# A planner's durations and yields rewritten for a streaming encoder layer: VectorE work issued in pieces

## The chip, the cores and the metric

The kernel runs on one core of a Trainium2 chip. A core has TensorE (PE; its weight loads are listed as PEld), VectorE (DVE), ScalarE (ACT), GpSimd (POOL) and SyncE (SP), which here only issues DMAs. Each engine works through its own instructions in order; semaphores make it wait for others. The metric is device time in microseconds (us), lower is better.

## What is computed

One layer on 1024 prompt rows and 64 sample rows of width 1024. A normalised input goes through one projection; its columns feed a differential attention (group A, 8 heads) and an RWKV-7 recurrence (group B, 16 heads of 64). Both are gated and go through one output projection. Cut to what matters:

```python
h = _rms_norm(x, norm_pre, NORM_EPS)
proj = h @ w_in
q = _partial_rope(proj[..., A_Q:A_K]...); k = _partial_rope(proj[..., A_K:A_V]...); v = proj[..., A_V:A_G]
s = jnp.einsum('bqhcd,bkhcd->bchqk', q, k) * (A_QK_DIM ** -0.5)      # two maps per head
p = jax.nn.softmax(where(visible, s, -inf), axis=-1)
o = (p[:, 0] - lam * p[:, 1]) @ v                                    # then rms norm, gate
ps = proj[..., B_R:B_G]
m = ps + (shifted_by_one_row(ps) - ps) * mu_shift                    # r, k, v, w, a of group B
def step(s, inp):                                                    # per head, state 64 x 64
    sa = jnp.einsum('bhij,bhj->bhi', s, a_t)
    s = s * w_t[:, :, None, :] + sa[..., None] * b_t[:, :, None, :] + v_t[..., None] * k_t[:, :, None, :]
    return s, jnp.einsum('bhij,bhj->bhi', s, r_t)
yb = group_norm(ys) * ln_x_w + ln_x_b + bonus                        # then gate
out = jnp.concatenate([y_a, yb], axis=-1) @ w_out
x_new = x + _rms_norm(out, norm_post, NORM_EPS)
```

## The kernel before

**Work.** The input is normalised and transposed first. Then `phase_b` runs the recurrence in 17 units: a pair of heads and one half of the prompt each (8 pairs x 2 halves), and the sample rows as one unit, put in as the last but one. A unit (`unit`, L485) prepares decays and keys (VectorE products on 128 x 512 tiles, the scan at L563), builds products of the chunks (`m_s`, L643 and L644, masked at L649 to L654), inverts a triangular matrix in five rounds (L690 to L715), then walks its 8 chunks in a serial chain (L812 to L865): a matmul g (L814), a VectorE copy (L828), a matmul u (L831), two copies (L837, L838), a matmul s (L842), and the update of the state in two halves (L852), from which the next chunk starts. Group norm, gate and a store of the result end the unit.

**Fillers.** Beside the units runs one stream of projections (`filler`, L996): 64 weight blocks of 128 columns, each 72 matmuls (`pj`, L215 to L217; every product is made of a high and a low part). Half of them (k, r, v, g for a pair of heads) are inputs of the units; after the matmuls of k, r and v, `shifted` (L362) mixes each row with the one before it, on ScalarE and VectorE. The other half (q, k, v, g of attention heads, `fill_job`, L942) goes to DRAM. `RESERVE` = 6 attention blocks are held back until the pairs are done. When the projections are done and phase B is over, the same stream becomes the output projection (`out_projection`, L1062; `po`, 864 matmuls of 512 columns, of which 216 need all heads).

**Attention.** `phase_a` (L1204) loads each head's q and k, splits them, and per query tile makes scores (`s`, L1361 and L1362, two buffers), the maximum (L1371), exponentials (L1378), transposes (`x_wt`, L1408) and sums (`x_o`, L1422).

**The order.** All of it is issued by `Weave` (L59), a planner that runs when the program is built. Each stream is a generator; it yields nanoseconds to wait or a condition, and `run` picks the lowest rank whose time has come: units by number, fillers at rank 100. TensorE time moves the clock by `spend`; `op` keeps for each other engine when it comes free and returns when its result is there. So a stream that waits longer in the model leaves more places for filler matmuls. Constants before: `LAT` = 100 ns after a matmul, a rate per element and a fixed 80 ns for each operation. Operations of fillers are not booked. The planner's order is then the order in which the instructions are scheduled onto each engine's queue.

Of the kernel before, what the change touches and what calls it, by code (L numbers as in the profile page):

```python
# [27 lines left out]
CH = 64  # L28
# [13 lines left out]
LA, LAT, W_LD, W_DMA = 130, 100, 11000, 3122  # L42
# [4 lines left out]
RS = 1.0  # L47
RATE = {DVE: 1 / 0.96, ACT: 1 / 1.2, POOL: 2.4}

# [6 lines left out]
b_done = [False]  # L56


class Weave:  # L59
# [7 lines left out]
    def __init__(self):  # L67
        self.now = 0.0
        self.live = []
        self.free = {}  # L70
        self.count = itertools.count()

    def spend(self, ns):
# [44 lines left out]
def layer(ctx: ExitStack, tc: tile.TileContext, I, O):  # L118
    nc = tc.nc
# [170 lines left out]
def phase_b(tc, I, O, E):  # L290
# [8 lines left out]
    with ExitStack() as bs:  # L299
# [62 lines left out]
        def shifted(w, idx, tag, dest):  # L362
# [5 lines left out]
        def shift(raw, idx, dest):  # L368
# [5 lines left out]
            for t0, n, d in dest:  # L374
                act(d, raw[:, t0 + 1:t0 + 1 + n], AF.Copy, scale=omu[:, idx:idx + 1])
                if t0 == TP:
                    stt(d[:, 0:1], pc(R_SS + idx), mu, d[:, 0:1], op0=MUL, op1=ADD)
                    stt(d[:, 1:], raw[:, t0 + 1:t0 + n], mu, d[:, 1:], op0=MUL, op1=ADD)
                else:
                    stt(d, raw[:, t0:t0 + n], mu, d, op0=MUL, op1=ADD)  # L380

# [22 lines left out]
        def pair_job(nm, p, w):  # L404
# [10 lines left out]
            if nm == "g":  # L415
                h0, h1 = yield from tiles()

                def evac(ps, t0, n):
                    for s0, s1, d in ((0, HALF, h0), (HALF, TP, h1), (TP, T, gs_[:, p, :])):
# [5 lines left out]
                        stt(d_, d_, 1.0, ps[:, a - t0:b - t0], op0=ADD, op1=MUL)  # L425
                yield from proj_cm(w, evac, f"g{p}")
            else:
# [6 lines left out]
                yield from shifted(w, 8 * j + p, f"{nm}{p}", dest)  # L434
            have.add((nm, p))
# [49 lines left out]
        def unit(n, p, hf):  # L485
# [66 lines left out]
            spend(1100)  # L552
# [10 lines left out]
            nc.vector.tensor_tensor_scan(cs, scm, tw, 0.0, op0=MUL, op1=ADD)  # L563
# [30 lines left out]
            done(op_(DVE, 560))  # L594
# [11 lines left out]
            for h in range(2):  # L606
                r = slice(64 * h, 64 * h + 64)
                vtt(pt[r, :, 2 + h, :], c3(rm)[r], dd[r, :, 1:CH + 1], op=MUL)
                vtt(pt[r, :, h, :], c3(kkn)[r], dd[r, :, 0:CH], op=MUL)
            stt(ta, ta, 1.0, kkn, op0=ADD, op1=MUL)  # L610
            stt(bk[:, :, CH:2 * CH], c3(ta), -0.5, c3(dinv), op0=MUL, op1=MUL)
            gtt(bk[0:64, :, 2 * CH:], c3(kb)[0:64], c3(dinv)[0:64], op=MUL)
            vtt(bk[64:128, :, 0:CH], c3(kb)[64:128], c3(dinv)[64:128], op=MUL)

            vtt(kb, kb, rm, op=MUL)
            op_(DVE, 512)
            free.add(("r", p, hf))
            op_(DVE, 4100)
# [18 lines left out]
            for g in range(2):  # L637
# [7 lines left out]
                spend(1800)  # L645
# [3 lines left out]
                vtt(lt[0:64, gs], pe3[0:64, :, 0:CH], bch(strict[0:64], 4), op=MUL)  # L649
                vtt(lt[64:128, gs], po3[64:128, :, 0:CH], bch(strict[64:128], 4), op=MUL)  # L650
                vtt(pt[64:128, gs, 0, :], pe3[64:128, :, 0:CH], bch(strict[64:128], 4), op=MUL)
                vtt(pt[0:64, gs, 1, :], po3[0:64, :, 0:CH], bch(strict[0:64], 4), op=MUL)
                vtt(rbk[:, gs, 0, :], pe3[:, :, CH:], bch(incl, 4), op=MUL)
                vtt(rbk[:, gs, 1, :], po3[:, :, CH:], bch(incl, 4), op=MUL)  # L654
                yield done(op_(DVE, 6 * 256 + 400), 2)
# [22 lines left out]
            for h in range(2):  # L678
                r = slice(64 * h, 64 * h + 64)
                vtt(c3(xt)[r], lt16[r, :, r], bch(mt[:, 0, :])[r], op=MUL)  # L680
            vtt(c3(xt), c3(xt), bch(id16), op=ADD)
            d = op_(DVE, 800)
            yield d
# [6 lines left out]
            for lv in range(1, 6):  # L690
# [4 lines left out]
                spend(300)  # L695
# [9 lines left out]
                spend(500)  # L705
# [15 lines left out]
            spend(500)  # L721
# [12 lines left out]
            spend(600)  # L734
# [7 lines left out]
            for h in range(2):  # L742
# [5 lines left out]
                spend(500)  # L748
# [27 lines left out]
            spend(500)  # L776
# [35 lines left out]
            for c in range(8):  # L812
# [41 lines left out]
                op_(DVE, 110)  # L854
                if c % 4 == 3:
# [7 lines left out]
                    op_(ACT, 400)  # L863
                    op_(ACT, 400)
                yield op_(DVE, 110)  # L865
# [4 lines left out]
            nc.vector.tensor_reduce(mu, y3, axis=AX.X, op=ADD)  # L870
            vts(mu, mu, -1.0 / CH, None, op0=MUL)
            yc = ycp[:, 0:HALF]
            vtt(c3(yc), y3, bcol(mu), op=ADD)
            yield op_(DVE, 1200)
# [9 lines left out]
            yield op_(POOL, 700)  # L884
# [49 lines left out]
            vtt(yo, yo, gate, op=MUL)  # L934
            if smp:
# [6 lines left out]
        def fill_job(kind, h, w):  # L942
# [3 lines left out]
            def evac(ps, t0, n):  # L946
                if kind == "g":
                    act(st_[:, t0:t0 + n], ps, AF.Tanh, scale=0.5)
                    stt(st_[:, t0:t0 + n], st_[:, t0:t0 + n], 1.0, ps, op0=ADD, op1=MUL)  # L949
                else:  # L950

                    act(st_[:, t0:t0 + n], ps, AF.Copy, scale=0.125 if kind == "q" else 1.0)
            yield from proj_cm(w, evac, f"a{kind}{h}")
# [9 lines left out]
        def rope(kd, g):  # L963
# [16 lines left out]
            for j in range(8):  # L980
# [543 lines left out]
```

## Time and profile before

| | us |
|---|---|
| median of 3 runs (1837.16 to 1842.88) | 1838.92 |
| the profiled execution | 1845.82 |
| its span, first to last instruction | 1844.0 |
| TensorE busy in the span | 1697.7 |
| VectorE busy in the span | 1254.7 |

The span is cut below into stretches by what runs: units and projections until 1229 us, the load of the first attention head until 1268, eight heads until 1714.7, the rest of the output projection. A busy TensorE is counted from the start of a matmul to its modelled end; the clock that is granted to it is in the same rows as a share of 2.4 GHz.

### The profile page before, as it was taken

The numbers are of one execution on the slowest core, as the hardware profiler recorded it, in microseconds if no ns is written. First come the engines' busy times: TensorE is split into PE (matmuls) and PEld (weight loads), VectorE is DVE, ScalarE is ACT, GpSimd is POOL, SyncE is SP. The second block draws the span as 40 slices with busy tenths as digits, with TensorE's granted clock in tenths as the row PEclk, the third lists the DMA queues.
The fourth block names the chain that finished last, engine by engine and source line by source line (L and its number), as shares of the span: only waits on it lengthen the run. The fifth ranks groups of instructions, "written<-read, shape, count | busy, mean of one in ns | idle before, by whom it ended". The sixth has DMA issues, their size and how long they took to land. (4 is left out here: it accounts for less than half of the span.)

```text
span 1844.0 us, 34363 instructions
## 1 busy us (share of the span) xinstructions
PE 1697.7 (92%) x12930; PEld 1516.1 (82%) x12930; DVE 1254.7 (68%) x2583; ACT 846.3 (46%) x2026; POOL 720.6 (39%) x905
## 2 busy tenths in 40 slices
PE   6999899899998999999999899997999988999997
PEld 4888898888888888888888789896889876777876
DVE  5677777778778787787776577643676655776336
ACT  5434444444443344344444334333466566676332
POOL 3542323233233233333333322212245466666663
PEclk8999999999999999999999899998999889999999
DMA  4111111320132111111111121346554654554345
GB/s 153 52 46 37 48 51 51 84 69 27 34 92 61 46 53 33 39 45 31 40 42 52 39 60 54 95 116 178 153 161 132 184 135 121 141 162 120 113 130 164
DMA packets 204096, 158.82 MB, mean 86 GB/s; under 512 B 44085, under 2 KB 185050, under 8 KB 203930
## 3 DMA queue, kind: packets, MB, share of 16 engines
q1 hardware_dynamic: 169098, 137.33, 26.0%
q10 hardware_dynamic: 34832, 19.30, 4.2%
q8 instruction: 102, 1.67, 0.4%
q14 instruction: 64, 0.52, 0.1%
HBM read 108.67 MB, written 47.34 MB: 85 GB/s over the span
## 5 line engine op out<-in xcount | busy, mean ns | idle before, releaser
L1183 PE MATMUL po<-woh,mxh 128*128 128x512 f32 x288 | 120.5, 418 | 2.7 <-ACT woh L157 1.9
L1184 PE MATMUL po<-woh,mxl 128*128 128x512 f32 x288 | 116.0, 403 | 4.1 <-POOL mxl L158 4.1
L1185 PE MATMUL po<-wol,mxh 128*128 128x512 f32 x288 | 115.1, 400 | 3.9 <-POOL wol L158 3.9
L1378 ACT ACTIVATE e<-s,nb 128x128 f32<-128x128 f32 (+7 forms) x144 | 101.1, 707 | 36.3 <-DVE nb L1371 20.5
L821 ACT ACTIVATE sd<-suv,dc 64x64 f32<-64x64 f32 x128 | 44.5, 347 | 151.4 <-DVE suv L852 138.1
L158 POOL TENSOR_TENSOR mxl<-mxr,mxh 128x512 fp32r<-128x512 f32 x63 | 84.5, 1344 | 66.1 <-ACT mxh L157 56.5
L1371 DVE TENSOR_REDUCE nb<-s 128x1 f32<-128x640 f32 (+8 forms) x104 | 95.9, 923 | 2.1
L1422 PEld LDWEIGHTS x_o<-vn,wt 128*128 128x128 f32 (+1 forms) x608 | 80.1, 198 | 15.1 <-ACT wt L1412 5.6
L1422 PE MATMUL x_o<-vn,wt 128*128 128x128 f32 (+1 forms) x608 | 86.5, 287 | 5.4 <-ACT wt L1412 4.1
L1361 PE MATMUL s<-k,qs 128*128 128x512 f32 (+4 forms) x208 | 77.9, 383 | 13.5 <-ACT k L1288 7.4
L842 PE MATMUL cbank<-suv,bkt 128*128 128x128 f32 x256 | 57.6, 307 | 32.0 <-DVE suv L838 31.9
L852 DVE SCALAR_TENSOR_TENSOR suv<-cbank,dc,sd 64x64 f32<-64x64 f32 x224 | 63.1, 282 | 32.7 <-PE cbank L842 28.7
L1194 DVE TENSOR_TENSOR part<-po,part 128x512 f32<-128x512 f32 x54 | 37.2, 689 | 67.2 <-PE po L1185 67.1
L842 PEld LDWEIGHTS cbank<-suv,bkt 128*128 128x128 f32 x256 | 41.9, 192 | 46.2 <-DVE suv L838 44.1
L215 PE MATMUL pj_v<-hhi,wh_v 128*128 128x384 f32 (+1 forms) x192 | 70.9, 369 | 6.2 <-DVE mg L425 5.8
L1362 PE MATMUL s<-k,qs 128*128 128x512 f32 (+4 forms) x208 | 72.0, 363 | 3.4 <-POOL k L1291 2.7
L687 POOL TENSOR_TENSOR ltlo<-lt,lt 64x512 f16<-64x512 f32 x32 | 38.0, 1186 | 93.5 <-ACT lt L675 92.3
L215 PE MATMUL pj_k<-hhi,wh_k 128*128 128x384 f32 (+1 forms) x192 | 67.8, 353 | 4.0 <-ACT raw_k L230 4.0
L215 PE MATMUL pj_r<-hhi,wh_r 128*128 128x384 f32 (+1 forms) x192 | 71.0, 370 | 0.0
L215 PE MATMUL pj_aq<-hhi,wh_aq 128*128 128x384 f32 (+1 forms) x192 | 70.3, 366 | 0.5 <-DVE fl_g L949 0.3
L215 PE MATMUL pj_av<-hhi,wh_av 128*128 128x384 f32 (+1 forms) x192 | 70.0, 364 | 0.7 <-DVE fl_g L949 0.7
L215 PE MATMUL pj_ak<-hhi,wh_ak 128*128 128x384 f32 (+1 forms) x192 | 70.2, 366 | 0.0
(532 smaller groups left out, 6079.7 us busy)
## 6 DMA issues: line engine op xcount, KB each, us to landing
mxr<-mixB SPq DMA_DIRECT2D x32, 256.0 KB
wor<-in_w_out SPq DMA_DIRECT2D x64, 128.0 KB
qa<-scr_q SPq DMA_DIRECT2D x32, 204.0 KB
ka<-scr_k SPq DMA_DIRECT2D x32, 204.0 KB
mxr<-mixA SPq DMA_DIRECT2D x24, 256.0 KB
scr_q<-fl_q SPq DMA_DIRECT2D x8, 544.0 KB
scr_k<-fl_k SPq DMA_DIRECT2D x8, 544.0 KB
scr_v<-fl_v SPq DMA_DIRECT2D x8, 544.0 KB
```

The source lines that it names most:

```text
L158: gtt(lo, raw, hi.bitcast(F32), op=SUB)
L215: mm(ps[:, :n], hi[:, k, :], hhi[i][:, k, :], start=(k == 0), stop=False)
L842: mm(s, bkt[:, c], suv[:, c], start=True, stop=True)
L852: stt(suv[r, c + 1, h, :] if c < 7 and not smp else to[r], s[r, h * CH:(h + 1) * CH], dc[r, c:c + 1], sd[r], op0=MUL, op1=ADD)
L1183: mm(ps, hi[:, q, :], wh, start=(q == 0), stop=False)
L1184: mm(ps, lo[:, q, :], wh, start=False, stop=False)
L1185: mm(ps, hi[:, q, :], wl, start=False, stop=(q == len(ks) - 1))
L1361: mm(s2[:, b:b + w], lq, k1[c][:, k0 + o_:k0 + o_ + w], start=True, stop=False)
L1362: mm(s2[:, b:b + w], lq, k2[c][:, k0 + o_:k0 + o_ + w], start=False, stop=True)
L1371: nc.vector.tensor_reduce(nb[:, 0:m], s3[:, :, 0:n], axis=AX.X, op=MAX, negate=True)
L1378: act(e[:, 0:n], s3[:, j, 0:n], AF.Exp, bias=nb[:, j:j + 1], accum_out=st["sm"][:, c:c + 1])
L1422: mm(ops[:, 0:P], wt[0:w, b, :], vn[0:w, vb, :], start=(b == 0), stop=(b == len(kbs) - 1))
```

## The change

It changes the planner's numbers and the places where streams yield; the operations stay, but for the scan, which becomes two halves, and one GpSimd product that is issued three instructions earlier.

- `LAT` becomes 210 ns, also in attention (`LA`, 130 before). `op` books a fixed part for each engine (`FIX`: 150, 190 and 90 ns) and adds `OUT` = 60 ns to its result. `spend` adds 130 or 105 ns when TensorE goes over to half-height matmuls or back. Several `spend` values change (450 to 1800 ns before; for `m_s` 1800 becomes 1400).
- `near` books an operation and lets the stream wait until VectorE is within 400 ns of it. It follows the single products of the preparation, of the masks, of the inversion's start, of the norm and of the rotation, where several were issued in one go.
- The mix with the row before is a stream of its own at rank 60 (`rest`), at most two of them open, and it yields after each operation. The evacuations of projections are booked.

```diff
-LA, LAT, W_LD, W_DMA = 130, 100, 11000, 3122
+LAT, OUT, W_LD, W_DMA = 210, 60, 11000, 3122
+LA = LAT
+T_IN, T_OUT = 130, 105
+FIX = {DVE: 150, ACT: 190, POOL: 90}
...
-    def op(self, eng, n):
-        self.free[eng] = max(self.now, self.free.get(eng, 0.0)) + RS * (RATE[eng] * n + 80)
-        return self.free[eng] - self.now + (LA if b_done[0] else LAT)
+    def op(self, eng, n, k=1, at=0.0):
+        self.free[eng] = max(self.now + at, self.free.get(eng, 0.0)) + RATE[eng] * n + k * FIX[eng]
+        return self.free[eng] - self.now + OUT
...
             nc.scalar.copy(raw[:, 1 + t0:1 + t0 + n], ps)
+            weave.op(ACT, n, at=LAT)
...
+        def shifted(w, idx, tag, dest, then):
+            yield lambda: len(shifting) < 2
+            shifting.append(tag)
             raw, evac = E["raw_rows"](tag)
             yield from proj_cm(w, evac, tag)
-            yield from shift(raw, idx, dest)
+            def rest():
+                yield from shift(raw, idx, dest, True)
+                shifting.remove(tag)
+                then()
+            weave.add(60, rest())
...
+        def near(eng, n):
+            return max(0.0, op_(eng, n) - OUT - 400)
...
-            nc.vector.tensor_tensor_scan(cs, scm, tw, 0.0, op0=MUL, op1=ADD)
+            nc.vector.tensor_tensor_scan(cs[:, 0:256], scm[:, 0:256], tw[:, 0:256], 0.0, op0=MUL, op1=ADD)
+            yield near(DVE, 512)
+            nc.vector.tensor_tensor_scan(cs[:, 256:], scm[:, 256:], tw[:, 256:], 0.0, op0=MUL, op1=ADD)
...
-                vtt(lt[0:64, gs], pe3[0:64, :, 0:CH], bch(strict[0:64], 4), op=MUL)
-                vtt(lt[64:128, gs], po3[64:128, :, 0:CH], bch(strict[64:128], 4), op=MUL)
...
-                yield done(op_(DVE, 6 * 256 + 400), 2)
+                for i, (o_, s_, m_) in enumerate((
...
+                    vtt(o_, s_, bch(m_, 4), op=MUL)
+                    yield near(DVE, 256) if i < 5 else done(op_(DVE, 256), 2)
```

VectorE, at the first chunks of the chain of unit (0, 1), where the masks of the next unit fall in. `gsb` is the copy of g, `suv` with COPY the copies of u, `suv` with SCALAR_TENSOR_TENSOR the update, `lt`, `pt` and `rbk` from `m_s` the six mask products; `mv` and `vs` are mixes of v, `ysq_o` the end of a unit. Before:

```order
L828 COPY gsb_10_2326<-cbank 128x128
L932 TENSOR_TENSOR ysq_o_0_2299<-ysq_o_0_2299,bv_0_1002 128x512
L380 SCALAR_TENSOR_TENSOR mv_1_2334<-raw_v_2027,pv,mv_1_2334 128x512
L377 SCALAR_TENSOR_TENSOR vs__501<-pv,vs__501 128x1
L378 SCALAR_TENSOR_TENSOR vs__501<-raw_v_2027,pv,vs__501 128x63
L934 TENSOR_TENSOR ysq_o_0_2299<-ysq_o_0_2299,mg_0_996 128x512
L649 TENSOR_TENSOR lt_0_2379<-m_s_00_2381,msk 64x256
L650 TENSOR_TENSOR lt_0_2379<-m_s_01_2382,msk 64x256
L651 TENSOR_TENSOR pt_508<-m_s_00_2381,msk 64x4x64
L652 TENSOR_TENSOR pt_508<-m_s_01_2382,msk 64x4x64
L653 TENSOR_TENSOR rbk_0_2380<-m_s_00_2381,msk 128x4x64
L654 TENSOR_TENSOR rbk_0_2380<-m_s_01_2382,msk 128x4x64
```

After (lines 868, 877, 878, 892, 694 and 402 are 828, 837, 838, 852, 649 to 654 and 380 of before):

```order
L868 COPY gsb_10_2462<-cbank 128x128
L877 COPY suv_1_2395<-cbank 64x64
L878 COPY suv_1_2395<-cbank 64x64
L892 SCALAR_TENSOR_TENSOR suv_1_2395<-cbank,dc_1_1233,sd_10_2459 64x64 x2
L402 SCALAR_TENSOR_TENSOR mv_0_2581<-raw_v_2319,pv,mv_0_2581 128x512
L868 COPY gsb_11_2515<-cbank 128x128
L877 COPY suv_1_2395<-cbank 64x64
L878 COPY suv_1_2395<-cbank 64x64
L694 TENSOR_TENSOR lt_0_2542<-m_s_00_2544,msk 64x256
L694 TENSOR_TENSOR lt_0_2542<-m_s_01_2545,msk 64x256
L892 SCALAR_TENSOR_TENSOR suv_1_2395<-cbank,dc_1_1233,sd_11_2512 64x64 x2
L694 TENSOR_TENSOR pt_508<-m_s_00_2544,msk 64x4x64
```

The six mask products stood in one piece between the copy of g and the copies of u; now they stand in pieces, behind the copies of u, and the update of the chunk goes between them.

TensorE, chunks six and seven of the last unit's chain, pair 7. `cbank` is g, u or s by its operands (`pt`, `xtf`, `bkt`), `y` the outputs. Before:

```order
L831 MATMUL cbank<-gsb_16_15098,xtf 128x128
L215 MATMUL pj_ak_1_15104<-hhi_174,wh_ak_14868 128x384
L216 MATMUL pj_ak_1_15104<-hlo_177,wh_ak_14868 128x384
L217 MATMUL pj_ak_1_15104<-hhi_174,wl_ak_14869 128x384
L215 MATMUL pj_ak_1_15104<-hhi_174,wh_ak_14868 128x384
L216 MATMUL pj_ak_1_15104<-hlo_177,wh_ak_14868 128x384
L217 MATMUL pj_ak_1_15104<-hhi_174,wl_ak_14869 128x384
L842 MATMUL cbank<-suv_1_14703,bkt_1_14672 128x128
L843 MATMUL y_14_14996<-suv_1_14703,rbk_1_14045 128x128
```

After (871, 882, 883, 854, 859 are 831, 842, 843, 814, 819 of before):

```order
L871 MATMUL cbank<-gsb_16_16094,xtf 128x128
L882 MATMUL cbank<-suv_1_15892,bkt_1_15861 128x128
L883 MATMUL y_14_16061<-suv_1_15892,rbk_1_15256 128x128
L854 MATMUL cbank<-suv_1_15892,pt_508 128x128
L859 MATMUL y_14_16061<-suv_1_15892,pt_508 128x128
L871 MATMUL cbank<-gsb_17_16108,xtf 128x128
L882 MATMUL cbank<-suv_1_15892,bkt_1_15861 128x128
L883 MATMUL y_14_16061<-suv_1_15892,rbk_1_15256 128x128
L937 MATMUL m_sto_10_16133<-ident,st_1_16115 64x128
L1317 MATMUL x_ck_16342<-ident,ck_455 128x128
```

The projections between the chain's matmuls are gone there; from the second chunk of this chain on none is left.

TensorE in the seventh attention head, from its first transpose. `x_wt` are transposes, `s` scores, `x_o` sums, `po` the output projection. Before:

```order
L1408 MATMUL x_wt_00_19758<-ident,e_000_19696 128x128
L1183 MATMUL po_19947<-woh_19561,mxh_19632 128x512
L1408 MATMUL x_wt_10_19761<-ident,e_100_19707 128x128 x2
L1184 MATMUL po_19947<-woh_19561,mxl_19633 128x512
L1446 MATMUL x_z_7_19789<-ident,on_4_19437 128x128 x3
L1361 MATMUL s_30_19784<-k_19518,qs_19485 128x512
L1362 MATMUL s_30_19784<-k_19548,qs_19485 128x512
L1361 MATMUL s_30_19784<-k_19585,qs_19550 128x512
L1362 MATMUL s_30_19784<-k_19610,qs_19550 128x512
```

After (1454, 1380, 1468, 1407, 1408 are 1408, 1334, 1422, 1361, 1362 of before):

```order
L1454 MATMUL x_wt_00_20714<-ident,e_000_20662 128x128
L1380 MATMUL x_kt_20716<-ident,ka_20139 128x64 x8
L1468 MATMUL x_o_0_20737<-vn_20151,wt_0_20713 128x128
L1407 MATMUL s_30_20744<-k_20579,qs_20575 128x512
L1408 MATMUL s_30_20744<-k_20596,qs_20575 128x512
L1407 MATMUL s_30_20744<-k_20611,qs_20598 128x512
L1408 MATMUL s_30_20744<-k_20624,qs_20598 128x512
L1454 MATMUL x_wt_10_20751<-ident,e_100_20673 128x128 x2
L1454 MATMUL x_wt_80_20800<-ident,e_800_20727 64x128
```

The output projection's matmuls no longer stand between the head's own. By head, from its first `x_vn` to that of the next, the matmuls of projections and of output projection were 231 + 0, 141 + 0, 120 + 0, 12 + 24, 0 + 84, 0 + 105, 0 + 75, 0 + 78 before, with 498 behind the last `x_o`; they are 0 + 192, 0 + 96, 0 + 108, 0 + 81, 0 + 90, 0 + 81, 0 + 0, 0 + 0 after, with 216 behind it.

## Rows read from the trace of the kernel before

**Rows 1.** The page's first part: busy us, share of the span, instructions.

```profile
PE 1697.7 (92%) x12930; PEld 1516.1 (82%) x12930; DVE 1254.7 (68%) x2583; ACT 846.3 (46%) x2026; POOL 720.6 (39%) x905
```

**Rows 2.** Busy time by stretch: length, then PE, PEld, DVE, ACT, POOL busy (instructions), clock, DMA.

```profile
100.00:1190.00 1090.00, 1025.94 (x9118) 932.71 (x9116) 819.63 (x1759) 454.38 (x1035) 342.22 (x408) 0.99 0.18 51
1190.00:1268.00 78.00, 65.54 (x399) 63.47 (x398) 31.09 (x79) 24.47 (x52) 15.70 (x16) 0.91 0.57 144
1268.00:1347.90 79.90, 73.54 (x434) 66.64 (x434) 48.38 (x101) 38.35 (x100) 33.73 (x40) 0.91 0.59 159
1347.90:1401.00 53.10, 52.04 (x351) 47.52 (x350) 34.10 (x68) 33.15 (x88) 26.70 (x38) 1.00 0.53 144
1401.00:1448.10 47.10, 46.99 (x323) 43.22 (x322) 32.91 (x69) 30.69 (x84) 19.97 (x31) 1.00 0.48 127
1448.10:1504.40 56.30, 45.27 (x243) 36.98 (x242) 33.48 (x70) 34.59 (x95) 30.77 (x41) 0.79 0.55 161
1504.40:1560.40 56.00, 48.43 (x289) 39.64 (x288) 34.16 (x68) 37.34 (x103) 34.87 (x47) 0.98 0.60 153
1560.40:1618.70 58.30, 54.32 (x312) 44.92 (x311) 38.76 (x75) 33.08 (x90) 36.26 (x48) 0.96 0.49 131
1618.70:1666.60 47.90, 46.15 (x282) 38.20 (x281) 36.27 (x69) 35.92 (x98) 33.08 (x42) 1.00 0.56 153
1666.60:1714.70 48.10, 44.98 (x273) 37.72 (x272) 32.09 (x65) 32.36 (x94) 31.55 (x47) 0.96 0.41 122
1714.70:1844.00 129.30, 116.27 (x504) 94.42 (x502) 54.54 (x71) 41.36 (x95) 70.11 (x76) 0.96 0.45 139
```

**Rows 3.** Waits of PE among the units, 100 to 1190 us: total, times, longest.

```profile
PE cbank L842 <- DVE suv L838: 31.9, 34, 3.4
PE cbank L831 <- DVE gsb L828: 10.0, 12, 1.8
```

**Rows 4.** Timeline, 205 to 208 us: start, us, engine, line, what [idle before, releaser].

```profile
205.18 0.41 DVE L649 TENSOR_TENSOR lt<-m_s,msk 64x256 f32<-64x256 f32 x1
...
207.38 0.21 DVE L837 COPY suv<-cbank 64x64 f32<-64x64 f32 x1
207.60 0.23 DVE L838 COPY suv<-cbank 64x64 f32<-64x64 f32 x1
207.88 0.49 PE L842 MATMUL cbank<-suv,bkt 128*128 128x128 f32 x2 [2.40 <-DVE suv L838]
```

**Rows 5.** Busy time by stretch, 1100 to 1190 us.

```profile
1100.00:1190.00 90.00, 89.26 (x831) 82.12 (x823) 58.75 (x135) 34.63 (x86) 18.80 (x17) 1.00 0.22 63
```

**Rows 6.** Timeline, end of the last chain to the first score.

```profile
1227.73 0.38 PE L831 MATMUL cbank<-gsb,xtf 128*128 128x128 f32 x2
1228.22 0.22 DVE L837 COPY suv<-cbank 64x64 f32<-64x64 f32 x1 [1.28 <-PE cbank L831]
...
1228.92 0.38 PE L842 MATMUL cbank<-suv,bkt 128*128 128x128 f32 x2
1229.35 0.58 DVE L852 SCALAR_TENSOR_TENSOR st<-cbank,dc,sd 64x64 f32<-64x64 f32 x2 [0.65 <-PE cbank L842]
...
1244.71 0.35 SPq L938 DMA_DIRECT2D mixB<-ysq_o  x1
...
1264.45 0.80 PE L1361 MATMUL s<-k,qs 128*128 128x128 f32 x2 [6.66 <-ACT k L1288]
```

**Rows 7.** Timeline of PE, two projection and two output matmuls that follow each other.

```profile
1179.80 0.34 PE L215 MATMUL pj_ak<-hhi,wh_ak 128*128 128x384 f32 x1
1179.97 0.34 PE L216 MATMUL pj_ak<-hlo,wh_ak 128*128 128x384 f32 x1
...
1715.25 0.39 PE L1183 MATMUL po<-woh,mxh 128*128 128x512 f32 x1
1715.47 0.39 PE L1184 MATMUL po<-woh,mxl 128*128 128x512 f32 x1
```

**Rows 8.** Busy time by stretch, 1452 to 1482 us.

```profile
1452.00:1482.00 30.00, 23.70 (x115) 18.32 (x113) 21.32 (x49) 18.86 (x54) 11.63 (x20) 0.77 0.75 225
```

More of the change, by code (lines that the diff above doesn't have):

```diff
@@ L70, in __init__, with spend @@
         self.free = {}
+        self.part = False
         self.count = itertools.count()
-    def spend(self, ns):
+    def spend(self, ns, part=False):
+        if part != self.part:
+            self.part = part
+            ns += T_IN if part else T_OUT
         self.now += ns
-    def op(self, eng, n):
-        self.free[eng] = max(self.now, self.free.get(eng, 0.0)) + RS * (RATE[eng] * n + 80)
-        return self.free[eng] - self.now + (LA if b_done[0] else LAT)
+    def op(self, eng, n, k=1, at=0.0):
+        self.free[eng] = max(self.now + at, self.free.get(eng, 0.0)) + RATE[eng] * n + k * FIX[eng]
+        return self.free[eng] - self.now + OUT
     def later(self, ns, call):
@@ L425, in evac @@
                         stt(d_, d_, 1.0, ps[:, a - t0:b - t0], op0=ADD, op1=MUL)
+                        op_(DVE, b - a, at=op_(ACT, b - a, at=LAT))
                 yield from proj_cm(w, evac, f"g{p}")
+                have.add((nm, p))
             else:
@@ L433, in dest @@
                     return [(0, HALF, h0[:, o_:o_ + HALF]), (HALF, HALF, h1[:, o_:o_ + HALF]), (TP, TS, samp)]
-                yield from shifted(w, 8 * j + p, f"{nm}{p}", dest)
-            have.add((nm, p))
+                yield from shifted(w, 8 * j + p, f"{nm}{p}", dest, lambda: have.add((nm, p)))
         def t512(tag="t", bufs=5, dt=F32, nm=""):
@@ L586, in unit @@
                 stt(kkn, km, pc(R_KK + p), psb, op0=MUL, op1=MUL)
+            yield near(DVE, 560)
+            done(0)
             kb = t512(nm=f"kb{u}")
@@ L608, in unit @@
                 vtt(pt[r, :, 2 + h, :], c3(rm)[r], dd[r, :, 1:CH + 1], op=MUL)
+                yield near(DVE, 512)
                 vtt(pt[r, :, h, :], c3(kkn)[r], dd[r, :, 0:CH], op=MUL)
+                yield near(DVE, 512)
+            gtt(bk[0:64, :, 2 * CH:], c3(kb)[0:64], c3(dinv)[0:64], op=MUL)
+            op_(POOL, 512)
             stt(ta, ta, 1.0, kkn, op0=ADD, op1=MUL)
+            yield near(DVE, 512)
             stt(bk[:, :, CH:2 * CH], c3(ta), -0.5, c3(dinv), op0=MUL, op1=MUL)
[L612 removed]
+            yield near(DVE, 512)
             vtt(bk[64:128, :, 0:CH], c3(kb)[64:128], c3(dinv)[64:128], op=MUL)
+            yield near(DVE, 512)
             vtt(kb, kb, rm, op=MUL)
[L616 removed]
+            yield near(DVE, 512)
             free.add(("r", p, hf))
[L618 removed]
             kbh = t512(dt=F32R, nm=f"kbh{u}")
@@ L680, in unit @@
                 vtt(c3(xt)[r], lt16[r, :, r], bch(mt[:, 0, :])[r], op=MUL)
+                yield near(DVE, 512)
             vtt(c3(xt), c3(xt), bch(id16), op=ADD)
-            d = op_(DVE, 800)
-            yield d
+            yield near(DVE, 256)
             nc.vector.transpose(x_, xt)
@@ L870, in unit @@
             nc.vector.tensor_reduce(mu, y3, axis=AX.X, op=ADD)
+            yield near(DVE, 512)
             vts(mu, mu, -1.0 / CH, None, op0=MUL)
@@ L985, in rope @@
                 vtt(a, a, tb[:, 0, :], op=MUL)
+                yield near(DVE, W)
                 vtt(b, b, tb[:, 1, :], op=MUL)
+                yield near(DVE, W)
                 vtt(a, a, b, op=ADD)
+                op_(DVE, W)
                 nc.sync.dma_start(out=E["rots"][kd, g, 2][:, cl], in_=a)
```

50 lines of the change are left out of this document (28 added, 22 removed).

## The prediction

> **What bounds the kernel now.** I read the page's first part, then busy time by stretch, then who ended TensorE's waits, then the timeline at two places. TensorE is busy 1697.7 of 1844.0 us, VectorE two thirds of the span [rows 1]. The profiled execution took 1845.82 us, 1.82 around its span, and lies 0.4% above the median of 1838.92; I sum the change against the span and carry the difference over to the median.
>
> Cut the span at the places where the work changes [rows 2]. From 100 to 1190 us the recurrent units run, woven with projections: TensorE idles 64.1 of 1090 us, and the granted clock, full at 2.4 GHz for most of it and at its lower level of 1.2 GHz after some gaps, averages 0.99, some 10 us more. From 1190 to 1268 us the last unit's chain and the load of the first attention head pass, still filled with projections. Then come eight heads of 47 to 80 us, and 129.3 us in which almost only the output projection is left.
>
> Of the idle time among the units, 41.9 us end with two VectorE copies of the chain [rows 3]. One case shows how: six mask products of about 0.42 us stand on VectorE, and the chain's two short copies come behind them, so TensorE stands 2.40 us [rows 4]. Where such rows stand further apart, 1100 to 1190 us, TensorE idles 0.74 of 90 us [rows 5].
>
> **What the change does to that.** No matmul is added or removed. 17 scans become two halves each. A copy of 64 columns takes 0.21 us [rows 4], the smallest VectorE instruction that the chain has; I price the second half's own start at no more, 17 x 0.21 = 3.6 us of VectorE, which has 270 of 1090 us to spare [rows 2]. I put it at 0; bounds 0 and 3.6 us. Moving one GpSimd product ahead of a VectorE one, and starting the mix with the previous token in a stream of its own, have the same cover: VectorE's spare time and the projection that runs on. If that cover is gone, a mix of two 512-element operations delays its unit by some 2 us; I add nothing.
>
> The order is the change. In the 136 chunks of the chains I summed what stands on VectorE between the copy of g and the copies of u, with the durations of the rows: 1.77 us in the mean before, 1.19 after; 71 chunks had over 1.5 us, now 40. What exceeds TensorE's own work in that hop falls from 78.7 to 23.5 us in sum. Between the copies and the state update it grows, from 2.5 to 7.5 us. Together 81 becomes 31. Beside that the planner puts about 261 projection matmuls into a unit in place of 212, so every hop has more cover.
>
> *First term, gain among the units.* At stake are 64.1 + 10 = 74 us. Bounds: if all stood as in the good stretch (0.8% idle), 1090 x 0.008 = 9 us stay; if only the hops' sums count (31 of 81), 38% or 28 us stay, and if the others don't move, 40. I take 20, nearer the good stretch, as the bursts are what that stretch lacks. Gain 54 us (34 to 65).
>
> *Second term, price at the end of the units.* All projections are now used up when the last chain has done its first chunk; before, 612 of 4680 were left when the last unit was transposed back. Seven chunks and a bit, 22 hops, stand without any other matmul. A hop's pieces: 0.49 us from a matmul's start to its copy, 0.45 for two copies of 0.22, 0.43 to the update, 0.58 for it [rows 6]; with the copy of g (0.49, and half the update's 0.58) and a semaphore's 0.05 before each matmul that is 2.9 us a chunk, of which TensorE works 0.5. 7.3 x 2.4 = 17.5 us idle. From the chain's last matmul to the first score there were 35.5 us: group norm, store of the result at +15.8, loads behind it, score at +35.5, with 6.66 us uncovered [rows 6]. Without projection weights being split between them I take 25 us, with 2 us of TensorE work: 23 idle. Before, the stretch 1190 to 1268 lost 12.5 us idle and some 6 us by the clock (0.91) [rows 2]. Price 17.5 + 23 - 18.5 = 22 us; 18 if norm and loads shrink further, 36 if they take the old 35.5 us and the clock is low throughout.
>
> *Third term, attention without projections.* A 384-column projection matmul starts every 0.175 us, an output one every 0.23 us [rows 7]; with a third of the tiles at 320 columns the projections' mean is 0.166 us. The second and third heads held 141 and 120 of them in 53.1 and 47.1 us, so a head's own work is 53.1 - 23.4 and 47.1 - 19.9, about 28.4 us [rows 2]. What each stretch took beyond its matmuls (231, 141, 120, 12 projections; 24, 84, 105, 75, 78 output matmuls; 498 at the end): 13.2, 1.3, -1.2, 20.4, 8.3, 5.7, 2.2, 1.8 and 14.8, in sum 66.5 us. After, the heads hold 192, 96, 108, 81, 90, 81, 0 and 0 output matmuls, and 216 come last. The start waits for output weights as well: 18. Five heads at 6 (between 8.3 and 1.8): 30. Two heads have nothing to fill: VectorE is busy 32.9 us in a head without output work, ScalarE 30.7 [rows 2], and in the nearest bare stretch, 1452 to 1482 us, VectorE reaches 71% [rows 8], so a bare head takes between 33 and 47 us; I take 41, since half of that stretch was at the low clock: 12.6 each. The end as before, 14.8. Sum 88, price 21 us. Bounds: -14 (bare heads at 33 us, the start at its old 13, five heads at 3) and +51 (heads of 47 us, start 25, others 8).
>
> Here a rule of the skill speaks against the change. The rows show that projections kept the heads at 47 to 53 us with TensorE full. The Trainium skill (Perfetto Trace Analysis, Optimization Strategy) says that regimes with different bottlenecks gain from being interleaved; by it, spending all projections in one regime costs the other the third term's upper bound: -54 + 22 + 51 = +19, 1858 us, the mechanism of the first rival. The trace agrees so far as the bare stretch goes.
>
> Sum: -54 + 22 + 21 = -11 us on 1838.9, so 1828 us.
>
> **The rivals.** *Bare heads cost more than the units gain* (slower). One mechanism: score, maximum, exponential and the freeing of one of two score buffers follow each other, and nothing else is on TensorE. Price +30 us on the third term and +14 on the second at their upper bounds, 1872 us; slower from bare heads of 49 us on, all else as above. For it: the bare stretch. Against: half of that was the opening of the output weights.
>
> *The clock stays low in bare heads* (slower). In 1448 to 1504 us, the only head with few fillers, the granted clock was 0.79 [rows 2]. If both heads ran at 1.2 GHz, 28.4 becomes 56.8 us of TensorE, 15.8 more than my 41: +32, 1860 us. The Trainium skill (TensorE: Matmul & The Clock Gate, Part 4) holds that transposes don't count as activity for the clock, and bare heads are rich in them. By that rule this rival holds; the trace shows the drop only beside real gaps.
>
> *The stall moves one hop* (slower). 39 chunks have over 1.5 us of VectorE work before the state update, 7 had. If these bind, the gain is 28 us: 1854.
>
> *Costs equal gains.* Within 5 us of zero: 1838. *The bursts don't spread:* the order shows that they do; a 0.02 chance that waits undo it, at 1838 too.
>
> **How the numbers follow.** A measurement of this kernel tells about 0.3%, 5.5 us, from no change. Forecast 0.46 (own range 1806 to 1833); costs equal gains 0.18; no spread 0.02; bare heads 0.17; clock 0.08; moved stall 0.09. So faster 0.46, within 0.3% 0.20, slower 0.34. The range, 1806 to 1868, reaches into each slower case and leaves out about 0.08 below (units near the good stretch and bare heads near 33 us) and 0.1 above.
>
> **What would show it.** TensorE's waits for the chain's copies fall from 42 to under 20 us, and the first score comes near 1316 us (1264.5 + 504 x 0.166 + 22 - 54, within 10). After it the span lasts about 517 us (579.5 - 84 + 21). The last chain shows eight chunks of about 3 us. Heads seven and eight take about 41 us each. Wrong would be waits that stay above 35 us, a first score past 1335, or bare heads past 49 us.

## The result

The kernel after takes 1926.89 us (median, 1922.97 to 1930.16), the kernel before 1839.97 beside it: ratio 1.0473, interval 1.0453 to 1.0494. It is 87 us slower; the prediction said 11 us faster, and its range ended at 1868.

The page's first part answers to [rows 1]: TensorE's work is the same 12930 matmuls, busy 15 us longer, in a span of 1924.6 us, 80.6 longer than before. The profiled execution of before lies 6 us above its median, so the two traces differ by 80.6 us where the medians differ by 87.

```profile
PE 1712.8 (89%) x12930; PEld 1521.4 (79%) x12930; DVE 1267.5 (66%) x2600; ACT 844.7 (44%) x2026; POOL 709.7 (37%) x905
```

Busy time by stretch of after, columns as in [rows 2]: units up to the last inversion, the last chain, the load of the first attention head, that head, the fourth head, the seventh.

```profile
100.00:1326.00 1226.00, 1150.23 (x9880) 1055.98 (x9878) 858.80 (x1838) 482.50 (x1090) 361.95 (x431) 0.99 0.21 59
1326.00:1370.70 44.70, 29.37 (x123) 22.14 (x123) 19.06 (x57) 8.13 (x24) 2.31 (x5) 0.59 0.07 20
1370.70:1393.10 22.40, 0.69 (x5) 0.22 (x3) 3.47 (x5) 7.72 (x13) 5.98 (x5) 0.50 0.90 223
1393.10:1487.60 94.50, 83.68 (x401) 67.60 (x402) 42.81 (x75) 50.51 (x127) 58.01 (x72) 0.86 0.49 141
1594.00:1664.10 70.10, 54.06 (x288) 44.34 (x287) 36.47 (x73) 34.87 (x98) 35.96 (x53) 0.88 0.46 129
1777.80:1824.10 46.30, 34.42 (x209) 27.82 (x209) 36.61 (x69) 29.19 (x80) 20.86 (x29) 0.92 0.35 86
```

Two things stand there. The units still idle 75.8 of 1226 us, 6.2% (5.9% before). And the end is empty: from 1326 us on TensorE lacks work, and from 1334 us on the full clock as well, until the first score at 1393.1.

To say where the 80.6 us are, time has to be freed of moved work. I cut each trace at the last unit's last inversion product (`m_iz`), at its last transpose back (`m_zt`) and at the first score, and add 0.166 us (the prediction's price) for each projection matmul that the order leaves behind the cut. What differs then is cost, not work that was moved. Each row is one profiled execution, so differences of some 6 us say nothing. The columns are the time to the first cut and between the cuts, and the time after the first score. Differences to before in us:

| kernel | run (us) | matmuls left at the cuts | units | last chain | load | attention |
|---|---|---|---|---|---|---|
| before (its own times) | 1839 | 816, 612, 504 | 1321.2 | 20.1 | 6.8 | 495.9 |
| after | 1926.9 | 18, 0, 0 | +7.8 | +21.7 | +15.5 | +35.6 |
| numbers only | 1927.2 | 150, 0, 0 | +22.2 | +7.2 | +16.3 | +31.2 |
| spread only | 1817.0 | 612, 405, 240 | -15.3 | -3.1 | -6.2 | -2.8 |
| after, fixed 80 ns | 1852.7 | 582, 363, 168 | +4.1 | 0.0 | -6.1 | +8.0 |
| after, reserve 18 | 1874.6 | 894, 666, 576 | +33.6 | -6.8 | +1.3 | -1.0 |
| after, reserve 13 | 1874.4 | 526, 282, 96 | +33.0 | -5.9 | -6.2 | +9.1 |
| before, fixed 150/190/90 | 1838.4 | 501, 276, 96 | -1.8 | -1.6 | -6.2 | +2.0 |
| before, subtraction on VectorE | 1816.5 | 816, 612, 504 | -23.9 | -3.7 | +0.4 | -0.2 |
| spread, subtraction on VectorE | 1786.5 | 612, 405, 240 | -44.3 | -3.9 | -6.2 | -2.1 |
| before, subtraction left out | 1796.7 | 816, 612, 504 | -39.6 | -3.6 | +1.7 | -7.5 |
| after, subtraction left out | 1875.1 | 18, 0, 0 | -43.1 | +21.7 | +16.7 | +31.2 |

So 72.8 of the 80.6 us are the end (21.7 + 15.5 + 35.6), and the units, which were to give 54, cost 7.8. The rows below the first two are taken up with the experiments; "spread" is the new order of issue with the old numbers, and the subtraction is GpSimd's, for the low part of the projections' weights.

The end, first the bare chain. Timeline of after, one chunk from matmul g to the next chunk's g (columns as in [rows 4]):

```profile
1345.96 0.80 PE L854 MATMUL cbank<-suv,pt 128*128 128x128 f32 x2 [0.27 <-DVE suv L892]
1346.79 0.29 DVE L868 COPY gsb<-cbank 128x128 f32<-128x128 f32 x1 [0.89 <-PE cbank L854]
1347.14 0.80 PE L871 MATMUL cbank<-gsb,xtf 128*128 128x128 f32 x2
1348.04 0.22 DVE L877 COPY suv<-cbank 64x64 f32<-64x64 f32 x1 [0.96 <-PE cbank L871]
1348.57 0.80 PE L882 MATMUL cbank<-suv,bkt 128*128 128x128 f32 x2 [0.64 <-DVE suv L878]
1349.40 0.60 DVE L892 SCALAR_TENSOR_TENSOR suv<-cbank,dc,sd 64x64 f32<-64x64 f32 x2 [0.89 <-PE cbank L882]
1350.06 0.80 PE L854 MATMUL cbank<-suv,pt 128*128 128x128 f32 x2 [0.26 <-DVE suv L892]
...
1393.08 0.80 PE L1407 MATMUL s<-k,qs 128*128 128x128 f32 x2 [21.71 <-ACT k L1334]
```

A chunk takes 4.10 us. Its three hops from a matmul's start to VectorE take 0.83, 0.90 and 0.83 us, where [rows 6] have 0.49 (twice, the first assumed alike) and 0.43: at 1.2 GHz each is 0.34 to 0.41 longer. The low clock lasts without a break from 1334.4 to 1409.5 us. The last row is the first score, after 21.71 us in which TensorE has nothing.

Who ended TensorE's waits among the units of after, 100 to 1326 us (us, times, longest), to be read beside [rows 3]:

```profile
PE cbank L882 <- DVE suv L878: 19.6, 18, 4.7
PE m_ip L734 <- DVE x L753: 15.4, 18, 2.9
PE m_iq L744 <- DVE q L738: 12.2, 14, 3.0
PE m_ix L760 <- DVE xt L748: 7.4, 8, 1.8
PE cbank L871 <- DVE gsb L868: 7.3, 14, 1.4
PE cbank L854 <- DVE suv L892: 6.2, 9, 1.5
```

Of before, 100 to 1190 us:

```profile
PE m_iq L704 <- DVE q L698: 4.5, 6, 1.9
PE cbank L814 <- DVE suv L852: 2.5, 3, 1.2
PE m_ip L694 <- DVE x L713: 0.8, 2, 0.6
```

The chain's copies did get better, 41.9 to 26.9 us. The inversion took it over: 35 us in the rows of `m_ip`, `m_iq` and `m_ix`, where before has 0.8 and 4.5 for the first two and no row for the third. (In both kernels the longest wait for a copy of u is not VectorE's doing. In after it ends at 1144.62 us after 4.66 us: ScalarE's queue issued 16 weight DMAs in a row from 1132.81 to 1143.16 us, and the copy waited for a ScalarE instruction, `sd`, behind them. In before it ends at 1031.05 us after 3.39, behind the same DMAs.) One wait of the inversion, `m_iq` at 1062.35 us after 3.03 us idle, on VectorE and GpSimd:

```profile
1057.56 2.70 POOL L167 TENSOR_TENSOR wl_v<-wr_v,wh_v 128x512 fp32r<-128x512 f32 x2
...
1057.63 1.50 DVE L589 COPY t_inx<-inv 128x512 f32<-128x512 f32 x1 [1.31 <-POOL inv L586]
1059.05 1.75 DVE L593 TENSOR_TENSOR_SCAN t_cs<-scm,t_th 128x256 f32<-128x256 bf16 x1
1060.72 0.66 DVE L595 TENSOR_TENSOR_SCAN t_cs<-scm,t_th 128x256 f32<-128x256 bf16 x1
...
1061.62 0.68 DVE L738 TENSOR_TENSOR q<-m_ip,mt 128x512 f16<-128x512 f32 x1
```

The two halves of the scan are the same instruction on the same size, yet the first takes 1.75 us and the second 0.66: the first ran while GpSimd subtracted two pieces of a projection's weights (`wl`, in `split`), the second after it. That holds for all 34 halves of this trace: the five that overlap a `wl` take 1.13 to 1.75 us, the other 29 take 0.65 to 0.69. The copy `t_inx`, 1.50 us here, takes 0.43 in the units where no `wl` runs beside it. The inversion's product `q` stands behind all that, and TensorE behind `q`. The Trainium skill (SBUF — State Buffer, Who interferes with whom) says that a VectorE instruction with two SBUF inputs contends with a GpSimd instruction that reads SBUF, the later one blocked until the earlier is done. The scan's rows agree; the copy, which has one input, is stretched in the same way.

Over all units I summed what VectorE's instructions took above the fastest fifth of their line, of those more than 30% and 60 ns above it: 78.6 us in before, 96.1 in after, of which 74.2 and 92.5 while GpSimd worked. Below this is called stretched time.

### The profile page after: what moved, and what is told of

It reads as the page before. It is cut to its first block, busy times and chain, and to the rows that moved or that the text cites. A ratio compares the mean times of both kernels' runs of the same rounds, so it can differ in the third digit from the quotient of the medians.

```text
span 1924.6 us, 34290 instructions
## 1 busy us (share of the span) xinstructions
PE 1712.8 (89%) x12930; PEld 1521.4 (79%) x12930; DVE 1267.5 (66%) x2600; ACT 844.7 (44%) x2026; POOL 709.7 (37%) x905
## 4 chain that ended last, share of the span: by engine, by line
PE 30%; DVE 10%; POOL 5%; DMA 4%; ACT 3%; issue 3%; SPq 0%; ACTq 0%; POOLq 0%; DVEq 0%
PE x_o L1468 3%; PE po L1231 2%; PE po L1230 2%; PE po L1229 2%; DMA wor<-in_w_out 1%; PE s L1407 1%; PE s L1408 1%; POOL mxl L167 1%; ACT e L1424 1%; PE x_wt L1454 1%; PE cbank L882 1%; PE cbank L871 1%; POOL qs L1331 1%; PE cbank L854 1%; PE pj_av L224 1%
## 5 line engine op out<-in xcount | busy, mean ns | idle before, releaser
L1468 PEld LDWEIGHTS x_o<-vn,wt 128*128 128x128 f32 (+1 forms) x608 | 81.8, 204 | 16.4 <-issue 4.0
L1230 PEld LDWEIGHTS po<-woh,mxl 128*128 128x128 f32 x288 | 57.1, 198 | 27.5 <-POOL mxl L167 18.0
L1407 PEld LDWEIGHTS s<-k,qs 128*128 128x128 f32 x208 | 41.6, 202 | 45.0 <-ACT k L1334 22.2
L727 POOL TENSOR_TENSOR ltlo<-lt,lt 64x512 f16<-64x512 f32 x32 | 37.8, 1180 | 100.9 <-ACT lt L715 99.7
L882 PEld LDWEIGHTS cbank<-suv,bkt 128*128 128x128 f32 x256 | 43.5, 197 | 37.7 <-DVE suv L878 34.7
L1229 PEld LDWEIGHTS po<-woh,mxh 128*128 128x128 f32 x288 | 56.6, 197 | 17.7 <-issue 4.1
```

The lines of the kernel that those rows point to most:

```text
L882: mm(s, bkt[:, c], suv[:, c], start=True, stop=True)
L1229: mm(ps, hi[:, q, :], wh, start=(q == 0), stop=False)
L1230: mm(ps, lo[:, q, :], wh, start=False, stop=False)
L1407: mm(s2[:, b:b + w], lq, k1[c][:, k0 + o_:k0 + o_ + w], start=True, stop=False)
L1468: mm(ops[:, 0:P], wt[0:w, b, :], vn[0:w, vb, :], start=(b == 0), stop=(b == len(kbs) - 1))
```

## The experiments

**The change in its two halves.** The order alone (after, with the old numbers):

```diff
-LAT, OUT, W_LD, W_DMA = 210, 60, 11000, 3122
+LA, LAT, W_LD, W_DMA = 130, 100, 11000, 3122
-FIX = {DVE: 150, ACT: 190, POOL: 90}
+FIX = {DVE: 80, ACT: 80, POOL: 80}
...
```

> The changed order of issue alone: the kernel after with the planner's old numbers (LAT 100, LA 130, 80 ns fixed per operation, LAT added to a result, no term for half-height matmuls, old spends, fillers' operations not booked); the waits between single VectorE operations, the halved scan and the mixing stream stay. By its order 240 projection matmuls are left at the first score (504 before, 0 after). Theory A (the numbers make the streams wait longer in the model, so that projections are spent among the units and the end stands bare): most of the loss is gone, 1835 to 1865 us. Theory B (the spreading itself costs, its single products delay the inversion and the chain): still 1890 us or more. Theory C (VectorE instructions stretched beside GpSimd make the stalls, wherever they stand): TensorE idles about 6% of the units' time here as in both others, and the time goes by what is left for the end, so near A.

1816.95 us, ratio 0.9886 (0.9862 to 0.991). B is out; it is better than A's range, as the units gained too, and theory C's 6% is missed: TensorE idles 54.0 of 1104.3 us there (4.9%). The numbers alone (before, with those lines the other way round, the new spends and the booked evacuations):

> The new numbers alone: the kernel before with LAT 210, OUT 60, FIX 150, 190 and 90 ns, the terms for half-height matmuls, the new spends and the fillers' evacuations booked; VectorE's products are issued in bursts as before, the scan is whole, the mix stays in the filler's stream. By its order no projection is left at the first score. Theory A: it loses nearly all that the change lost, 1905 to 1950 us. Theory B: within 1% of before, 1825 to 1860. Theory C: as A, and TensorE's idle share among the units near 6% (5.9% before, 6.1% after).

1927.21 us, ratio 1.0488 (1.0457 to 1.0519): the whole loss, as theory A has it. TensorE idles 82.4 of 1218.4 us among the units (6.8%). As in after, its load stands bare:

```profile
1370.70:1393.90 23.20, 0.64 (x4) 0.17 (x2) 3.49 (x5) 7.65 (x13) 5.96 (x5) 0.50 0.90 221
```

**Which number.** `FIX` back to 80 in after, and the new `FIX` alone in before (`RATE[eng] * n + {DVE: 150, ACT: 190, POOL: 90}[eng]`):

> One line of the kernel after undone: the fixed part of an operation is 80 ns for each engine again in place of 150, 190 and 90. By its order 168 projection matmuls are left at the first score, and the last unit's chain still has some between its matmuls. Theory A: the end is paid back, 1840 to 1875 us; the first score comes within 25 us of 1265 + (504-168) x 0.166 = 1321 us. Theory B: the order is spread as in after, so it stays at 1900 us or more.

> One number alone put into the kernel before: the fixed part of an operation is 150 ns on VectorE, 190 on ScalarE and 90 on GpSimd in place of 80. By its order 96 projection matmuls are left at the first score (504 before, 0 after). Theory A (this number spends the projections early): slower than before by a large part of the loss, 1865 to 1915 us, with idle time among the units no lower than 60 us. Rival (the number needs the other ones with it to lose): within 15 us of before.

Undone in after: 1852.73 us (1.0079, 1.005 to 1.0108), 74 us back, with the first score at 1318.1 us. Alone in before: 1838.40 us (0.9994, 0.9984 to 1.0005), so it costs nothing, and theory A is wrong there: 408 matmuls fewer are left at the first score than in before, and the end costs no more. The last chain and the load of that run:

```profile
1236.20:1292.00 55.80, 52.33 (x346) 50.32 (x346) 30.44 (x83) 18.64 (x46) 14.46 (x15) 0.97 0.36 101
1292.00:1322.50 30.50, 30.50 (x186) 30.36 (x185) 5.76 (x7) 10.59 (x18) 6.94 (x8) 1.00 0.81 221
```

TensorE is busy 52.33 of 55.8 and 30.5 of 30.5 us. So A must be put otherwise: with 96 matmuls left at the first score the end costs no more than with 504, and with none left it does; no run lies between 96 and none. All numbers together use up everything, `FIX` alone does not. That run also holds some 234 projection matmuls in a unit (4242 behind the first unit's inversion less 501 behind the last one's, over 16 units) in place of 214 and idles 63.9 us among the units, before 64.1: more fillers in a unit did not shorten its waits.

**The end alone.** After with `RESERVE` 18 and 13 in place of 6:

> The kernel after with RESERVE 18 in place of 6: 18 of the attention's projection blocks are held back until the pairs' blocks are done, and by its order 576 matmuls are left at the first score, and heads hold 273, 147, 141, 15 of them, about as before. All else as after. Theory A: the time after the last unit is that of before (579.5 us from the first score); what the reserve takes from the units may come back there as bare hops: 1840 to 1885 us. Theory B: the units lose as in after, so 1900 us or more.

> The kernel after with RESERVE 13 in place of 6. By its order 282 projection matmuls are left at the last unit's last transposes and 96 at the first score, every head but the last holds 93 to 111 others, and one unit in the middle has about 32 fillers in place of 260. Theory A (the bare end is some 50 us of the loss): idle time from the last chain's end to the first score falls from 27.7 to under 10 us, the run to 1865 to 1892 us. Rival (the loss is in the units, the end only shows it): 1900 us or more.

With 18 it takes 1874.55 us (1.0201, 1.0175 to 1.0228), with 13 1874.42 us (1.0185, 1.0158 to 1.0213). Chain, load and attention together cost 72.8 us above before in after and -3.0 here with 13, so the bare end is worth 76 us. The reserve pays 25 of them in the units, where one unit has 32 fillers. Idle time among the units is no longer for it (74.8 us with 13, 75.8 in after), but the clock is low for 68 us among them, 24 in after. In the trace of 18, from one unit's inversion to the next, units with 249 to 285 fillers idle 2.3 to 4.9 us each, those with 113 to 184 idle 3.4 to 6.5, and the one with 32 idles 12.7: a hundred fillers fewer cost a unit some 1.5 us of idle time, and only the nearly empty one lost more.

**GpSimd beside VectorE.** The weights' subtraction left out, in before and in after:

```diff
-            split(hi[:, j:j + 4, :], lo[:, j:j + 4, :], raw)
+            nc.scalar.copy(hi[:, j:j + 4, :], raw)
+            nc.scalar.copy(lo[:, j:j + 4, :], raw)
```

> The kernel before with GpSimd's subtraction for the projections' weights left out: the low part of a weight block is a second ScalarE copy of the weights in its place (so the projections' products are other numbers), and GpSimd has nothing to do with the weights. In the trace of before VectorE's instructions among the units take 78.6 us more than the fastest fifth of their line, and 74.2 us of that while GpSimd works, 35.7 beside this subtraction. Theory C (VectorE's instructions stretched beside GpSimd make much of the stalls): that excess falls below 50 us, TensorE's idle time among the units from 64 us to 50 or less, the run to 1815 to 1832 us. Rival (the stalls come from bursts and hops, and stretched instructions stand elsewhere): idle time stays within 6 us of 64, the run within 6 us of before.

> The same edit on the kernel after: the low part of a weight block is a ScalarE copy, GpSimd's subtraction is left out. There the excess is 96.1 us, 60.2 of it beside this subtraction, and TensorE idles 73.4 us until the last chain. Theory C: excess below 50 us, idle time below 50 us, the run 20 to 40 us shorter (1887 to 1907), since after has more of its waits behind such instructions than before. Rival: idle time within 6 us of 73, the run within 6 us of 1927.

Before without it takes 1796.68 us (0.9767, 0.9742 to 0.9792), after without it 1875.07 us (1.019, 1.0157 to 1.0223): 42 and 52 us less, more than theory C asked. Stretched time is 44.5 and 39.3 us, idle time among the units 40.2 and 43.5. TensorE's waits among the units of after without it:

```profile
PE cbank L883 <- DVE suv L879: 14.3, 15, 4.8
PE m_ix L761 <- DVE xt L749: 7.5, 8, 1.8
PE m_ip L735 <- DVE x L754: 5.2, 10, 2.0
PE m_iq L745 <- DVE q L739: 4.2, 10, 0.9
```

The inversion's waits fall from 35.0 to 16.9 us, so about half of them come with that subtraction. Without it both orders idle alike, and the units of after are only 3.5 us cheaper than those of before (-43.1 and -39.6 in the table): the subtraction raises the idle time of both orders, but without it the new order with the new numbers gains nothing among the units either.

Then nothing left out, the subtraction on VectorE (`vtt(lo[...], raw, hi[...], op=SUB)`), on before and on the spread order:

> The kernel before with the subtraction for the projections' weights on VectorE in place of GpSimd, nothing left out: 128 more instructions of about 0.65 us on VectorE, 83 us in all. Theory C (GpSimd's work beside VectorE's sets the stalls): most of the 42 us that leaving it out gave remain, 1800 to 1825 us. Rival (VectorE's own load sets them): slower than before, 1840 to 1870, by bursts in the chain's hops.

> The changed order with the old numbers (1817 us) and the subtraction on VectorE in place of GpSimd, nothing left out. Theory C: 1785 to 1808 us. Rival (VectorE's own load sets the stalls): 1817 to 1850 us.

On before it takes 1816.48 us (0.9876, 0.9858 to 0.9893), on the spread order 1786.49 us (0.9711, 0.969 to 0.9732), though VectorE has 128 instructions more. Stretched time is 38.7 and 33.1 us, idle time 47.2 and 37.8. The second is faster than both kernels of this case; its waits among the units:

```profile
PE cbank L880 <- DVE suv L876: 8.7, 19, 1.3
PE cbank L852 <- DVE suv L890: 8.7, 9, 1.2
PE cbank L869 <- DVE gsb L866: 5.6, 6, 2.3
PE m_zt L954 <- DVE ycp L923: 5.0, 6, 1.2
PE m_ip L732 <- DVE x L751: 2.2, 4, 1.1
```

The first half of the scan, mean 895 ns in after, is 683 here, the second 702 and 675 (groups of 15 halves each, after and then this run):

```profile
L593 DVE TENSOR_TENSOR_SCAN t_cs<-scm,t_th 128x256 f32<-128x256 bf16 x15 | 13.4, 895 | 0.2
L595 DVE TENSOR_TENSOR_SCAN t_cs<-scm,t_th 128x256 f32<-128x256 bf16 x15 | 10.5, 702 | 0.1
...
L591 DVE TENSOR_TENSOR_SCAN t_cs<-scm,t_th 128x256 f32<-128x256 bf16 x15 | 10.3, 683 | 0.0
L593 DVE TENSOR_TENSOR_SCAN t_cs<-scm,t_th 128x256 f32<-128x256 bf16 x15 | 10.1, 675 | 0.1
```

The subtraction in four pieces, still on GpSimd, does not fit so well:

```diff
-            split(hi[:, j:j + 4, :], lo[:, j:j + 4, :], raw)
+            nc.scalar.copy(hi[:, j:j + 4, :], raw)
+            for q in range(j, j + 4, 1):
+                gtt(lo[:, q:q + 1, :], raw[:, q - j:q - j + 1, :], hi[:, q:q + 1, :].bitcast(F32), op=SUB)
```

> The kernel of the changed order with the old numbers (1817 us), and GpSimd's subtraction of the projections' weights in four pieces of 128 columns in place of one of 512, nothing left out. If a VectorE instruction is held up by the one GpSimd instruction that it meets (about 1.3 us here), pieces of a quarter hold it up less: excess from 72 us to under 50, the run 1800 to 1813 us. Rival (VectorE is slow for as long as GpSimd works, in pieces or not): excess 65 us or more, the run 1813 to 1825 us, since each piece has a start of its own.

1818.65 us (0.9882, 0.9862 to 0.9903). Stretched time fell from 72.4 to 40.7 us as the first half said, and the run not at all. So the gain of taking the subtraction off GpSimd is shown; that the stretched instructions are all of its mechanism is not. What else it frees (GpSimd's own queue) stays open.

**What spreading is worth.** One number varied where it should hardly matter (80 ns fixed, in the order before and in the spread order), and the masks alone spread (a wait behind each of the first five products of before):

```diff
                 vtt(lt[0:64, gs], pe3[0:64, :, 0:CH], bch(strict[0:64], 4), op=MUL)
+                yield max(0.0, op_(DVE, 256) - LAT - 400)
```

> The kernel of the changed order with the old numbers, and 60 ns in place of 80 as the fixed part of an operation. By its order 360 projection matmuls are left at the first score in place of 240, and heads hold 151, 113 and 96 of them. Theory A (what is left for the end is what pays there): 1805 to 1817 us, since two heads more are filled; if the units lose cover by it, their idle time rises over 60 us and the run stays at 1815 to 1825.

> A control: the kernel before with 70 in place of 80 ns as the fixed part of an operation, nothing else; by its order as many projection matmuls are left at the first score as in before (504). Theory S (spreading itself gains some 20 us): this stays within 8 us of before, 1832 to 1848. Theory L (the order's detail is a lottery: small changes of a number move the run by 10 to 20 us, and the 23 us that spreading alone gained are one draw of it): it may lie 10 us or more off in either direction, 1815 to 1860.

> The changed order with the old numbers and 70 in place of 80 ns (360 matmuls left at the first score, as with 60 ns, which took 1835 us). Theory S: 1810 to 1828 us. Theory L: anywhere in 1815 to 1850, and TensorE's idle time among the units anywhere between 50 and 75 us.

> The changed order with the old numbers and 90 in place of 80 ns (168 matmuls left at the first score). Theory A (fewer left for the end cost) with S: 1820 to 1838 us, 3 to 15 more than with 80 ns. Theory L: anywhere in 1815 to 1850.

> The kernel before with one part of the spreading: the planner's stream waits between the six mask products (five waits), all else as before. In before the waits for the chain's copies cost 41.9 us among the units, and the six products stood in front of the copies in the case that the prediction showed. If these bursts make the waits: idle time among the units from 64 to 50 us or less, the run 1815 to 1830. Rival (the waits come from stretched instructions and other work, the masks are a small part): idle time 58 us or more, the run within 8 us of before.

In the same order: spread with 60 ns 1834.86 us (0.9983, 0.9965 to 1.0001; outside both of its spans), before with 70 ns 1845.67 us (1.0033, 1.0011 to 1.0054), spread with 70 ns 1860.48 us (1.0119, 1.0078 to 1.0159; outside both theories' spans), spread with 90 ns 1824.00 us (0.9934, 0.9913 to 0.9955), and the masks alone 1835.77 us (0.9986, 0.997 to 1.0002). The spread order takes 1835, 1860, 1817 and 1824 us at 60, 70, 80 and 90 ns: the 23 us of the first run are one draw of a wide scatter. The masks, on whose burst [rows 4] rested, move idle time among the units from 64.1 to 59.1 us and the run by nothing. With the subtraction on VectorE:

> The changed order with the old numbers, 70 ns as the fixed part (1860 us with the subtraction on GpSimd) and the subtraction on VectorE. If the scatter comes from where VectorE meets GpSimd, this gains more than the 30 us that 80 ns gained: 1785 to 1815 us. If the scatter is the order's own: 1822 to 1845, about 30 us less than 1860.

> The same with 90 ns (1824 us with the subtraction on GpSimd). Either theory: 1780 to 1800 us; below 1786 it is the fastest so far.

With 70 ns it takes 1807.80 us (0.9832, 0.9816 to 0.9849), with 90 ns 1793.61 us (0.9758, 0.9744 to 0.9773). Over 70, 80 and 90 ns the scatter falls from 43 to 21 us, and all three spread orders now lie 9 to 30 us below the 1816.5 of the order before. Three draws do not show how much of the scatter comes from where VectorE meets GpSimd's subtraction; that the order has scatter of its own without it, they do.

## Why the prediction was wrong

**First term, -54, measured +7.8 up to the last inversion.** This is the step that failed: 62 of the 98 us between the forecast of -11 and the 87 measured. It took the waits of [rows 3] for the effect of bursts, counted the hops' sums with usual durations, and let idle time fall to the good stretch's. The direction was right for the chain, whose copies' waits fell by 15 us to 26.9, between the "under 20" and the "above 35" that it named. But it summed no hop of the inversion, where single products now stand between two steps and TensorE's waits rose from about 5 to 35 us. And it overlooked that the durations vary: an instruction of 0.66 us takes 1.75 beside GpSimd, which a model with a fixed duration does not see; half of the inversion's waits go with the subtraction. Why the other half stands there, and why the new order gains nothing without the subtraction, stays open. The good stretch [rows 5] may not have been a fair measure either: GpSimd is busy 18.80 of its 90 us, against 28.3 in 90 us over all units [rows 2], so it differs by more than its spacing, and no run separates the two. The second leg, that 261 fillers in a unit cover more than 212, fell with the fixed part alone in before. The rival "the stall moves one hop" had the direction, with the wrong hop: the update's waits are 6.2 us (2.5 before), the inversion's 35.

**Second term, +22, measured +37.2.** The mechanism was right, the price of a chunk was not: 2.9 us against 4.10, all of it in the low clock, which the term left to its upper bound (36). The way from the chain's last matmul to the first score took 31.9 us where I took 25 and bounded by 35.5. The first score came at 1393.1 us, where the prediction had 1316 and named 1335 as a sign of being wrong.

**Third term, +21, measured +35.6.** Of its pieces, the start (18) measured 90.9 - 28.4 - 192 x 0.23 = 18.3, the two bare heads 46.3 and 34.4 us against 41 each, the end 16.4 against 14.8. Five heads at 6 us were 30 and measured 43.4, of which the fourth has 23.1 and the fifth 13.2. There the output projection's mix halves came late from GpSimd, for 13.0 us, and the clock averaged 0.88 and 0.95. Waits of TensorE in these two heads:

```profile
PE po L1230 <- POOL mxl L167: 13.0, 4, 7.0
```

Sum of the second and third: 73 in place of 43. Neither the rival of bare heads (from 49 us on) nor that of their clock (0.92 in the seventh, 0.95 in the eighth) decided. The Trainium skill (Perfetto Trace Analysis, Optimization Strategy), which the prediction cited, says that interleaving regimes may help. By it the prediction put this term at its upper bound, 51; the traces point the same way, with 35.6 where nothing is left, and 2.0 and 9.1 where 96 matmuls are.

**The place of the numbers.** I treated the change as one. The half that I thought of as mere bookkeeping, the numbers, makes all of the loss, and the half that I priced, the order, makes anything between 23 us lost and 23 gained.

## What to carry to other kernels

Where a planner's waits are filled from a limited store, look first at when the store runs out: with 96 of 4680 matmuls left at the first score the end lost nothing, and with none left it lost 55 us (numbers only) to 73 us (after), since the chain, the load and the heads stood bare one after the other. A longer booked duration spends that store whether or not it meets a real wait: `FIX` alone took it from 504 to 96 and left the idle time as it was. And before work is spread on an engine, compare its longest and shortest durations of one instruction: if they differ two and a half times, look at the other engine at work beside it. Moving that work gave 23 to 53 us here, where spreading alone gave no sure gain.

## What was not expected of the hardware

A scan of 128 x 256 took 0.66 us alone and 1.75 beside GpSimd's subtraction; halving the 512 scan itself cost about 0.14 us (two halves of 0.68 and 0.67 against the 1.22 of before). The clock stayed at 1.2 GHz for 75 us in one piece, through the bare chain's matmuls, the load, in which TensorE had almost nothing, and 16 us of the first head.
